# A first weight block on GpSimd's queue, and four small loads moved behind a weight chunk

## The chip, the cores and the metric

One core of a Trainium2 chip runs the whole kernel. The metric is device time in microseconds (us) of one execution. Before the change it was 484.42 us, the median of 3 runs (484.12 to 484.95).

The engines that matter here: TensorE (PE) multiplies, ScalarE (ACT) and VectorE (DVE) prepare its operands, SyncE (SP) and GpSimd (POOL) issue DMAs, each on a queue of its own.

## What is computed

One decoder layer on 256 positions of width 1024: an input projection feeds an mLSTM branch and an attention branch, both are gated, summed and projected, and a gated MLP follows. The start of the kernel, where the change sits, computes the output gate `o` of the mLSTM branch and the input and forget gate columns, which are columns of the input projection:

```python
proj = jnp.einsum("bsd,dn->bsn", x, w_in) + b_in
q_m, k_m, v_m, o_m, i_m, f_m, q_b, k_b, v_b, g_a, g_b = _split_cols(proj, SPLIT_SIZES)
...
y_a = (jax.nn.sigmoid(o_m.astype(jnp.float32)) * head_norm(h_m, mlstm_norm)).astype(x.dtype)
...
bias_own = jnp.moveaxis(rel_bias[t5_bucket(rel_own)], -1, 0).astype(jnp.float32)
```

## The kernel before

Float32 precision is reached by splitting every operand into a high part (`h`, type fp32r, a cast on ACT, line 93) and a low part (`l`, the rest, a subtraction on DVE, line 94) and multiplying three times: high by high, low by high, high by low (`split_into` and `mm3`). So every weight and input block goes through four hands: a DMA, ACT, DVE, PE.

The weights come as chunks of 1 MB (`wst[s]`, 128 x 2048), in the order of `chunk_order`: chunks 0 to 3 are the output gate's, then from chunk 4 on the projections of the queries, keys and so on (4 is the first queries' chunk, `qm`; 5 is `qb`, 6 `km`, 7 `kb`), and after 36 chunks of projections and gates come those of the later stages. `load(s)` issues the whole chunk s on SP's queue into one of three rotating buffers `raw`; `split_parts(s)` cuts it into high and low tiles `wh`, `wl`; `step_<kind>` multiplies.

The output gate is special, because nothing is loaded yet when it starts. Its four chunks and the transposed input are loaded in pieces, in the order in which PE uses them, in a loop over the eight slices k of 128 input features. For each k: one slice of the input (`xraw`, 128 KB); one piece of chunk 2 (into the tile `sgb`) and one of chunk 3 (into `sigo`), each 128 KB for k = 0 to 3 and 256 KB for k = 4 and 6; and one block of 256 KB of chunk 0 or 1 (into `raw`; for chunk 1 the split halves are called `yah` and `yal`). PE computes in `step_o`, for each k, the products of chunk 2's piece (`ps_o2a`, `ps_o2b`), chunk 3's with the gate columns `wif` (`ps_o3a`, `ps_o3b`) and the 512 columns of chunk 0 or 1 (`ps_o0a`, `ps_o0b`); for k = 0 and 1 in that order. ACT and DVE work through the casts and subtractions in a fixed order too, so a late piece holds up those behind it.

SP issues DMAs strictly in order. Its DMAs share eight completion semaphores (`DMAHW0` to `DMAHW7` in the rows below), so from the ninth on each waits for the landing of one about eight places ahead of it. POOL's queue has semaphores of its own (`DMASW`).

Behind the loop POOL broadcasts two bias rows (`bo`, `bvm`, lines 251 and 252), which wait for a load of SP's queue, and then issues four small loads: `rel` (the bias table, 2 KB as loaded), `onehot` (64 KB), `ident` (the identity for transposes, 64 KB) and `vec` (biases, convolution taps and gains, 138 KB). After them SP loads chunks 4 to 8.

`rel_split` casts `rel` and `onehot` (lines 283 to 285). From them `rel_bias_expand` makes, by one matmul (`ps_rel`, line 558), a table of the relative position bias in DRAM (`ev`, lines 562 and 563, then `table`), which is read back as `toe` for the attention's logits (line 777). `side_pe[s]` holds small PE work that is run right behind step s, `side_elem[s]` small ACT and DVE work that `elem_work(s)` runs ahead of step s. `vec` is first used by ACT at line 463, `ident` by the transposes into `ps_gt` (line 585).

Of the kernel before, what the change touches and what calls it, by code (L numbers as in the profile page):

```python
# [19 lines left out]
S = 256  # L20
# [52 lines left out]
class Kernel:  # L73
# [105 lines left out]
    def run(self):  # L179
        tc, nc, ctx = self.tc, self.nc, self.ctx  # L180
# [29 lines left out]
        ident = const.tile([P, P], F32, name="ident")  # L210
        vec = const.tile([P, NV], F32, name="vec")
        rel = xp.tile([2 * NB, 8], F32, name="rel")
        onehot = xp.tile([2 * NB, S], F32, name="onehot")
# [13 lines left out]
        raw = [self.stream.tile([P, 2048], F32, tag="raw", name=f"raw{s}", bufs=3) for s in range(2)]  # L227
# [6 lines left out]
        dma = nc.sync.dma_start  # L234
        cut = [(k // 4, slice(k % 4 * 512, k % 4 * 512 + 512)) for k in range(KT)]
        pieces = {0: 1, 1: 1, 2: 1, 3: 1, 4: 2, 6: 2}
        for k, (s, c) in enumerate(cut):
            dma(xraw[:, k], self.xt_d[:, k])
            for t in (2, 3, s) if k < 2 else (2, s, 3):
                if t == s:  # L240
                    dma(raw[s][:, c], self.wst[s, :, c])
                elif k in pieces:
                    d = slice(k * 256, (k + pieces[k]) * 256)
                    dma(raw[t][:, d], self.wst[t, :, d])
                if t == 3 and k == 0:
                    dma(self.wif, self.wif_d)
            if k == 3:

                dma(brow.rearrange("p (a d) -> p a d", a=2), self.rows_d[0:2, :].unsqueeze(0))
                dma(bif, self.bif_d.to_broadcast([P, 8]))  # L250
        nc.gpsimd.partition_broadcast(bo, brow[:, 0:D])
        nc.gpsimd.partition_broadcast(self.bvm, brow[:, D:2 * D])
        twice = (2, NB)
        for t, d in ((rel, self.rel_d.unsqueeze(0).to_broadcast([*twice, 8])),
                     (onehot, self.onehot_d[:, 0:S].unsqueeze(0).to_broadcast([*twice, S])),
                     (ident, self.ident_d), (vec, self.vec_d)):
            nc.gpsimd.dma_start(t, d)


        v3 = [t.rearrange("p (k f) -> p k f", k=KT) for t in whl[3]]  # L260
        for k, (s, c) in enumerate(cut):
# [4 lines left out]
            d = slice(k * 256, (k + n) * 256)  # L266
# [12 lines left out]
        both = xp.tile([2 * NB, 8], F32R, name="relhl")  # L279
        oneh = self.ybl.rearrange("p k s -> p (k s)")[0:2 * NB, 0:S]  # L280
# [6 lines left out]
        for s in range(4, 9):  # L287
            if s == 7:
                self.split(4)
            self.load(s)  # L290
        g = nc.gpsimd


# [27 lines left out]
        self.pst = {}  # L321


        self.rel_bias_expand(both, oneh)
        self.gates_schedule(bif)
        for gi in range(NG):
            self.group_schedule(gi)
# [7 lines left out]
        ffn_cm = tc.tile_pool(name="ffn", bufs=1)  # L335
        ahead_cm = tc.tile_pool(name="ahead", bufs=1, side="right")
        first = {k: self.order.index((k, 0)) for k in ("wa", "wo", "up")}
        for f in [self.gate_sums] + self.o_sums + [rel_split]:
            f()
        self.split(5)  # L340
        for s, (kind, i) in list(enumerate(self.order))[4:]:
# [207 lines left out]
        self.step_gate(s, "gb", g, V_BGB)  # L549


    def rel_bias_expand(self, rel, onehot):
        nc = self.nc
        st = {}

        def pe():
            st["ps"] = ps = self.ps_side([8, S], "ps_rel")
            nc.tensor.matmul(ps, rel, onehot, start=True, stop=True)

        def elem():  # L560
            ev = self.xp.tile([8, LTOE], F32, name="ev")
            nc.vector.tensor_scalar(ev[:, P:LTOE], self.backward(st["ps"]), 1.0 / ATT_SCALE, None, op0=ALU.mult)
            nc.vector.memset(ev[:, 0:P], NEG)
            nc.gpsimd.dma_start(self.table, ev)
            self.load_band(0)
        self.side_pe.setdefault(4, []).append(pe)
        self.side_elem.setdefault(5, []).append(elem)


    def gates_schedule(self, bif):  # L570
# [727 lines left out]
```

## Time and profile before

| | before |
|---|---|
| median of 3 runs | 484.42 us |
| the profiled execution | 485.31 us |
| its span, first to last instruction | 483.6 us |
| PE busy | 474.1 us |
| granted TensorE clock | 0.995 |

The time of the profiled execution is 1.7 us longer than its span: what lies ahead of the first and behind the last instruction. Rows of the timeline give the start in us, the duration, the engine, the line of the code, the operation with output and input tiles, and in square brackets how long the engine had stood idle just before and what released it. `SPq` is SP issuing a DMA. Tiles of one name are told apart by time: `raw` is the tile of chunk 0 before 11 us, of chunk 1 until 25 us, of chunk 4 behind that.

### The profile page before, as it was taken

To read this page: it belongs to the slowest core of one execution; us is meant where nothing else is said; L and a number is where in the kernel's file an instruction comes from. 1 tells how busy PE (TensorE), PEld (TensorE's weight loads), DVE (VectorE), ACT (ScalarE), POOL (GpSimd) and SP (SyncE) were. 2 spreads that over 40 slices of the span, in tenths; PEclk is the share of its full clock that TensorE was granted. 3 is DMA by queue.
4 is the path that set the end of the run, shared out by engine and by line. 5 is a ranking of instruction groups with operands and counts; after the bars stand their busy time and mean duration, and the time that the engine had idled before them with its cause. 6 is when DMAs were issued, how large, how long until landed. Compare 5 with 4: busy or idle time off the path is not lost.

```text
span 483.6 us, 9414 instructions
## 1 busy us (share of the span) xinstructions
PE 474.1 (98%) x3831; PEld 458.8 (95%) x3831; DVE 371.1 (77%) x666; ACT 297.9 (62%) x509; POOL 23.7 (5%) x41
## 2 busy tenths in 40 slices
PE   7999999999999999999999999999999999999994
PEld 5989999999999999999999999999999999999984
DVE  5779986886689668986677798888768767767886
ACT  5479777586667756866655632767456544555871
POOL 0500002000100010002000001000000000000000
PEclk9999999999999999999999999999999999999998
DMA  7976655364637453743954491837454655456202
GB/s 226 286 303 223 220 198 197 127 237 170 192 103 264 175 169 114 272 170 106 380 219 173 175 344 41 298 102 260 176 194 166 232 194 182 172 205 222 90 1 89
DMA packets 18214, 92.70 MB, mean 192 GB/s; under 512 B 2475, under 2 KB 5433, under 8 KB 8313
## 3 DMA queue, kind: packets, MB, share of 16 engines
q1 hardware_dynamic: 16714, 87.61, 50.3%
q0 software_dynamic: 1456, 4.49, 3.4%
q8 instruction: 30, 0.49, 0.4%
q14 instruction: 14, 0.11, 0.1%
HBM read 91.02 MB, written 1.06 MB: 190 GB/s over the span
## 4 chain that ended last, share of the span: by engine, by line
PE 92%; DMA 5%; DVE 1%; ACT 1%; SPq 1%; issue 0%; DVEq 0%; ACTq 0%
PE ps_up L147 25%; PE ffn L147 13%; PE ps_ga L147 5%; PE ps_kb L147 5%; PE ps_qb L147 5%; PE ps_gb L147 5%; PE ps_vm L147 5%; PE mix L147 5%; PE ps_vb L147 5%; PE ps_wb L147 5%; PE ps_wa L147 5%; PE ps_km L147 4%; PE ps_qm L147 4%; DMA raw<-in_wst_dram 2%; DMA sigo<-in_wst_dram 1%; PE psn L147 1%
## 5 line engine op out<-in xcount | busy, mean ns | idle before, releaser
L94 DVE TENSOR_TENSOR wl<-raw,wh 128x1024 fp32r<-128x1024 f32 (+4 forms) x147 | 180.3, 1264 | 26.3 <-ACT wh L93 23.5
L93 ACT CAST wh<-raw 128x1024 fp32r<-128x1024 f32 (+4 forms) x147 | 151.6, 1080 | 7.9 <-DMA raw<-in_wst_dram 5.6
L147 PE MATMUL ps_up<-x1h,wl 128*128 128x256 f32 x320 | 88.5, 276 | 0.0
L147 PE MATMUL ps_up<-x1h,wh 128*128 128x256 f32 x320 | 88.5, 276 | 0.0
L147 PE MATMUL ps_up<-x1l,wh 128*128 128x256 f32 x320 | 88.4, 276 | 0.0
L147 PEld LDWEIGHTS ps_up<-x1l,wh 128*128 128x128 f32 x320 | 60.1, 188 | 0.4
L147 PEld LDWEIGHTS ps_up<-x1h,wh 128*128 128x128 f32 x320 | 60.1, 188 | 0.3
L147 PEld LDWEIGHTS ps_up<-x1h,wl 128*128 128x128 f32 x320 | 60.1, 188 | 0.0
L1076 DVE SCALAR_TENSOR_TENSOR cu<-ps_up,vec,cu 128x255 f32<-128x255 f32 (+1 forms) x80 | 33.1, 476 | 20.4 <-ACT cu L1072 20.4
L147 PE MATMUL ffn<-wh,hl 128*128 128x512 f32 (+2 forms) x94 | 35.5, 378 | 0.0
L147 PE MATMUL ffn<-wl,hh 128*128 128x512 f32 (+2 forms) x94 | 35.5, 377 | 0.0
L147 PE MATMUL ffn<-wh,hh 128*128 128x512 f32 (+2 forms) x94 | 35.3, 375 | 0.0
L93 ACT CAST hh<-cu 128x256 fp32r<-128x256 f32 x22 | 8.9, 406 | 40.4 <-DVE cu L1087 40.4
L1072 ACT ACTIVATE cu<-ps_up,vec 128x256 f32<-128x256 f32 x40 | 16.7, 469 | 22.5 <-PE ps_up L147 22.5
L147 PEld LDWEIGHTS ffn<-wh,hl 128*128 128x128 f32 x94 | 17.7, 188 | 3.2
L147 PEld LDWEIGHTS ffn<-wl,hh 128*128 128x128 f32 x94 | 17.7, 188 | 3.1
L147 PEld LDWEIGHTS ffn<-wh,hh 128*128 128x128 f32 x94 | 17.7, 188 | 3.0
L147 PE MATMUL ps_qm<-xth,wl 128*128 128x256 f32 x64 | 17.9, 280 | 0.4 <-DVE wl L94 0.4
L147 PE MATMUL ps_qm<-xth,wh 128*128 128x256 f32 x64 | 18.0, 281 | 0.0
L147 PE MATMUL ps_ga<-xth,wh 128*128 128x256 f32 x64 | 18.0, 281 | 0.0
L147 PE MATMUL mix<-wh,mgh 128*128 128x256 f32 x64 | 17.8, 279 | 0.0
L147 PE MATMUL ps_qb<-xth,wh 128*128 128x256 f32 x64 | 17.8, 278 | 0.0
(343 smaller groups left out, 1444.6 us busy)
## 6 DMA issues: line engine op xcount, KB each, us to landing
raw<-in_wst_dram SPq DMA_DIRECT2D x77, 1024.0 KB, 4.9
raw<-in_wst_dram SPq DMA_DIRECT2D x8, 256.0 KB, 4.4
lnrow<-in_rows_dram POOLq DMA_DIRECT2D x4, 512.0 KB, 7.0
xraw<-in_xt_dram SPq DMA_DIRECT2D x8, 128.0 KB, 4.0
toe<-table POOLq DMA_DIRECT2D x4, 256.0 KB, 5.3
xtok<-in_x_dram POOLq DMA_DIRECT2D x1, 1024.0 KB, 8.1
sgb<-in_wst_dram SPq DMA_DIRECT2D x4, 128.0 KB, 3.9
sigo<-in_wst_dram SPq DMA_DIRECT2D x4, 128.0 KB, 3.7
```

The lines of the kernel that those rows point to most:

```text
L93: self.nc.scalar.copy(wh, raw)
L94: self.nc.vector.tensor_sub(wl, raw, wh.bitcast(F32))
L147: self.nc.tensor.matmul(ps, a[i], b[i], start=start and i == 0, stop=stop and i == 2)
L1072: act.activation(cu[:, j, :], ps[:, j, :], AF.Copy, scale=tap(2, j))
L1076: v.scalar_tensor_tensor(cu[:, j, o:], ps[:, j, :S - o], tap(t, j), cu[:, j, o:], op0=ALU.mult, op1=ALU.add)
```

## The change

Three edits. The block of k = 0 of chunk 0 (256 KB) is issued by POOL instead of SP. The four small loads leave POOL's queue: SP issues `vec` and `ident` behind chunk 4 and `rel` and `onehot` behind chunk 5. And, as `rel` and `onehot` come later, `rel_split` moves from ahead of step 4's loop into `elem_work(4)`, the matmul of `ps_rel` from behind step 4 to behind step 5, and the table's evacuation from step 5 to step 6.

```diff
             for t in (2, 3, s) if k < 2 else (2, s, 3):
                 if t == s:
-                    dma(raw[s][:, c], self.wst[s, :, c])
+                    (dma if k else nc.gpsimd.dma_start)(raw[s][:, c], self.wst[s, :, c])
...
         twice = (2, NB)
+        small = [(vec, self.vec_d), (ident, self.ident_d)]
         for t, d in ((rel, self.rel_d.unsqueeze(0).to_broadcast([*twice, 8])),
-                     (onehot, self.onehot_d[:, 0:S].unsqueeze(0).to_broadcast([*twice, S])),
-                     (ident, self.ident_d), (vec, self.vec_d)):
-            nc.gpsimd.dma_start(t, d)
+                     (onehot, self.onehot_d[:, 0:S].unsqueeze(0).to_broadcast([*twice, S]))):
+            small.append((t, d))
...
             self.load(s)
+            if s < 6:
+                for _ in range(2):
+                    dma(*small.pop(0))
...
-        self.rel_bias_expand(both, oneh)
+        self.rel_bias_expand(both, oneh, rel_split)
...
-        for f in [self.gate_sums] + self.o_sums + [rel_split]:
+        for f in [self.gate_sums] + self.o_sums:
             f()
...
-        self.side_pe.setdefault(4, []).append(pe)
-        self.side_elem.setdefault(5, []).append(elem)
+        self.side_elem.setdefault(4, []).append(split)
+        self.side_pe.setdefault(5, []).append(pe)
+        self.side_elem.setdefault(6, []).append(elem)
```

What it moves, at three places. First SP's queue at the very start; `raw0` is the tile of chunk 0. Before:

```order
L238 DMA xraw_88<-in_xt_dram 128x256
L244 DMA sgb_101<-in_wst_dram 128x256
L244 DMA sigo_106<-in_wst_dram 128x256
L246 DMA wif_98<-in_wif_dram 128x64
L241 DMA raw0_107<-in_wst_dram 128x512
L238 DMA xraw_88<-in_xt_dram 128x256
L244 DMA sgb_101<-in_wst_dram 128x256
L244 DMA sigo_106<-in_wst_dram 128x256
L241 DMA raw0_107<-in_wst_dram 128x512 [waits DMAHW0_49]
```

The same place on SP with the change:

```order
L238 DMA xraw_88<-in_xt_dram 128x256
L244 DMA sgb_101<-in_wst_dram 128x256
L244 DMA sigo_106<-in_wst_dram 128x256
L246 DMA wif_98<-in_wif_dram 128x64
L238 DMA xraw_88<-in_xt_dram 128x256
L244 DMA sgb_101<-in_wst_dram 128x256
L244 DMA sigo_106<-in_wst_dram 128x256
L241 DMA raw0_107<-in_wst_dram 128x512
L238 DMA xraw_88<-in_xt_dram 128x256 [waits DMAHW0_49]
```

The fifth DMA is gone from SP's list and everything behind it stands one place further ahead. It now heads POOL's list, in front of the broadcasts, and the four small loads are gone from there:

```order
L241 DMA raw0_107<-in_wst_dram 128x512
L251 ISA
L251 ISA bo_91<-sga_100 128x1024 [waits DMAHW0_49]
L252 ISA bvm_92<-sga_100 128x1024
L264 COPY xfirst_99<-xth_89 128x128 [waits Activation_49]
```

Second, SP's queue at the end of the output gate's loads, where the last block of chunk 1 (`raw1`) is followed by the chunks 4, 5, 6; with the change:

```order
L241 DMA raw1_108<-in_wst_dram 128x512 [waits DMAHW5_49]
L88 DMA raw4_358<-in_wst_dram 128x2048 [waits DMAHW6_49]
L293 DMA vec_95<-in_vec_dram 128x276 [waits DMAHW7_49]
L293 DMA ident_94<-in_ident_dram 128x128 [waits DMAHW0_49]
L88 DMA raw5_362<-in_wst_dram 128x2048 [waits DMAHW1_49,DMASW0_49,DVE_49]
L293 DMA rel_96<-in_rel_dram 64x1x8 [waits DMAHW2_49]
L293 DMA onehot_97<-in_onehot_dram 64x1x256 [waits DMAHW3_49]
L88 DMA raw6_366<-in_wst_dram 128x2048 [waits DMAHW5_49,DMAHW4_49,DVE_49]
```

Before, chunks 4, 5 and 6 stood here one behind the other; the four L293 rows are new.

Third, PE behind step 4 (`ps_qm0` is chunk 4's product, `ps_qb0` chunk 5's). Before:

```order
L147 MATMUL ps_qm0_437<-xth_89,wl4_369 128x256
L558 MATMUL ps_rel_486<-ybl_105,relhl_211 8x256 [waits DVE_49,PE_49,Activation_49]
L585 MATMUL ps_gt_488<-ident_94,gt_411 4x128 [waits DMASW2_49,PE_49]
L585 MATMUL ps_gt_488<-ident_94,gt_411 4x128 x3
L147 MATMUL ps_qb0_526<-xth_89,wh5_421 128x256 [waits Activation_49]
L147 MATMUL ps_qb0_526<-xtl_90,wh5_421 128x256
L147 MATMUL ps_qb0_526<-xth_89,wl5_422 128x256 [waits DVE_49]
```

With the change:

```order
L147 MATMUL ps_qm0_437<-xth_89,wl4_369 128x256
L589 MATMUL ps_gt_486<-ident_94,gt_411 4x128 [waits DMAHW0_49,DVE_49]
L589 MATMUL ps_gt_486<-ident_94,gt_411 4x128 [waits DVE_49]
L589 MATMUL ps_gt_486<-ident_94,gt_411 4x128 x2
L147 MATMUL ps_qb0_519<-xth_89,wh5_418 128x256 [waits DVE_49,PE_49,Activation_49]
L147 MATMUL ps_qb0_519<-xtl_90,wh5_418 128x256
```

The matmul of `ps_rel` has left this place; it stands 48 matmuls later, between chunk 5's and chunk 6's products. The lines behind the diff's third place are numbered three or four higher in the changed kernel.

More of the change, by code (lines that the diff above doesn't have):

```diff
@@ L549, in step_gb, with rel_bias_expand @@
         self.step_gate(s, "gb", g, V_BGB)
-    def rel_bias_expand(self, rel, onehot):
+    def rel_bias_expand(self, rel, onehot, split):
         nc = self.nc
```

## The prediction

> **What bounds the kernel now.** The page first: busy times, the chain that ended last, and the costliest issues.
>
> ```profile
> PE 474.1 (98%) x3831; PEld 458.8 (95%) x3831; DVE 371.1 (77%) x666; ACT 297.9 (62%) x509; POOL 23.7 (5%) x41
> ...
> PE 92%; DMA 5%; DVE 1%; ACT 1%; SPq 1%; issue 0%; DVEq 0%; ACTq 0%
> ```
>
> PE is busy 98% of the span and carries 92% of the chain. So the question is where PE stands still. The view of waits, asked for PE alone, answers with three rows for the whole execution:
>
> ```profile
> PE warm_ps L201 <- DVE warm L198: 1.3, 1, 1.3
> PE ps_o0a L427 <- ACT wh L93: 1.2, 1, 1.2
> PE ps_qm L147 <- DVE wl L94: 0.4, 1, 0.4
> ```
>
> The first is the start, which the change doesn't touch. The other two, 1.2 and 0.4 us, both lie in the first 31 us and are all that earlier loads can win. After the second, PE runs without a wait until its last product; time won or lost by then is carried to the end unchanged. The timeline shows the first wait:
>
> ```profile
> 2.65 0.43 SPq L241 DMA_DIRECT2D raw<-in_wst_dram  x1
> 4.55 0.40 ACT L93 CAST wh<-sigo 128x256 fp32r<-128x256 f32 x1
> 5.82 0.29 PE L427 MATMUL ps_o3b<-wl,xth 128*128 128x264 f32 x1
> 6.61 0.62 ACT L93 CAST wh<-raw 128x512 fp32r<-128x512 f32 x1 [1.66 <-DMA raw<-in_wst_dram]
> 7.29 0.50 PE L427 MATMUL ps_o0a<-wh,xth 128*128 128x512 f32 x1 [1.18 <-ACT wh L93]
> ```
>
> The block of k = 0, issued by SP at 2.65 as its fifth DMA, lands at about 6.6; ACT has waited 1.66 for it and PE starts 0.68 after the cast starts. This is the block that POOL is to load. What comes behind is tight as well, as the chain of waits says, which runs backward through DMAs, not PE, up to 27 us:
>
> ```profile
> 3.13 3.82 DMA xraw<-in_xt_dram
> ...
> 11.68 6.08 DMA sigo<-in_wst_dram
> ...
> 18.15 9.20 DMA raw<-in_wst_dram
> ...
> 29.58 1.23 DVE wl L94
> ```
>
> Each landing lets SP issue the next of these. The last is chunk 4, landing at 27.35; its last low half is ready at 30.81 and PE, which has arrived 0.35 earlier, goes on at 30.85. So a gain at 7.29 is kept only if the blocks between and chunk 4 come earlier too.
>
> **The block of k = 0.** SP's first issue, and the first DMA that POOL issues before:
>
> ```profile
> 0.81 0.38 SPq L238 DMA_DIRECT2D xraw<-in_xt_dram  x1
> 14.51 1.00 POOL L257 DMA_DIRECT2D rel<-in_rel_dram  x1
> ```
>
> A common start releases all engines, so I take 0.8 us for POOL's issue too. The landing on POOL's queue at that time is not in the trace, so it is bounded, from the views of DMA issues in narrow windows (the last figure is us from issue to landing):
>
> ```profile
> raw<-in_wst_dram SPq DMA_DIRECT2D x1, 256.0 KB, 3.9
> toe<-table POOLq DMA_DIRECT2D x1, 256.0 KB, 3.7
> vec<-in_vec_dram POOLq DMA_DIRECT2D x1, 138.0 KB, 7.1
> rel<-in_rel_dram POOLq DMA_DIRECT2D x1, 2.0 KB, 6.0
> ```
>
> The best case is `toe`, as large and on POOL's queue, at 48 us, when few loads were under way: 0.8 + 3.7 = 4.5. The worst is `vec`, on the same queue in the thick of the loads: 0.8 + 7.1 = 7.9. The nearest row is the block itself, which took 3.9 on SP's queue among these very neighbours. I add the longer issue of POOL's first DMA, 1.00 - 0.43 = 0.57: 0.8 + 3.9 + 0.57 = 5.3. Then PE could go on at 5.3 + 0.68 = 6.0, right behind the row at 5.82, and the wait of 1.18 is gone.
>
> Not all of it is taken. The 16 DMA engines are shared, and this is how busy they were (windows view; the last two columns are the DMA share and GB/s):
>
> ```profile
> 2.00:4.50 2.50, 2.50 (x8) 1.03 (x6) 0.84 (x2) 1.00 (x4) 0.00 (x0) 1.00 0.81 212
> 4.50:5.60 1.10, 1.10 (x11) 1.09 (x10) 0.66 (x3) 0.45 (x2) 0.00 (x0) 1.00 0.68 148
> 5.60:12.40 6.80, 5.62 (x36) 4.89 (x35) 4.62 (x11) 4.59 (x12) 0.33 (x1) 1.00 0.93 310
> 17.10:27.40 10.30, 10.30 (x67) 9.24 (x66) 5.75 (x10) 5.13 (x10) 1.14 (x8) 1.00 1.03 350
> ```
>
> Free engine time is 0.19 x 2.5 + 0.32 x 1.1 = 0.83 us ahead of 5.6; the block needs 256 KB at 310 GB/s, 0.85 us. It about fits, but while it runs it takes turns with `sigo`, whose cast at 4.55 leads to products at once. I take off 0.3: **a gain of 0.9 us at this place**, between 1.2 (all) and a loss of 7.9 + 0.68 - 7.29 = 1.3.
>
> The Trainium skill, in "DMA: Bandwidth & Descriptors", section "Issuing engines are not separate DMA queues", says that DMAs of several issuing engines run on the same 16 DMA engines, so that issuing from more of them saves only the sequencer's time. The shares of 0.81 and 0.68 above agree that the engines were largely taken; the issue time saved is one slot, 3.13 - 2.65 = 0.48 us, and by the rule alone the sum here would be 0.48 in place of 0.9. The same page's fit for a DMA of this queue (section "Anatomy of one DMA — SWDGE (gpsimd) path") would give, as an estimate, 2.0 + 0.6 = 2.6 us to landing; the 3.7 of `toe` is longer and is used.
>
> **Does the gain hold?** Every later piece is issued a slot of 0.48 earlier, and 0.83 us of engine time is newly used ahead of 5.6, so I take 0.7 us for the landings behind, between 0 and 0.83. The tight ones, and the row that frees a buffer for chunk 6:
>
> ```profile
> 17.07 0.62 ACT L93 CAST yah<-raw 128x512 fp32r<-128x512 f32 x1 [1.99 <-DMA raw<-in_wst_dram]
> 17.89 0.39 PE L427 MATMUL ps_o0a<-yah,xth 128*128 128x512 f32 x1
> 24.71 0.69 DVE L94 TENSOR_TENSOR wl<-sigo,wh 128x512 fp32r<-128x512 f32 x1 [1.27 <-ACT wh L93]
> 25.46 0.39 PE L427 MATMUL ps_o3a<-wl,xth 128*128 128x264 f32 x1
> 25.66 0.69 DVE L94 TENSOR_TENSOR yal<-raw,yah 128x512 fp32r<-128x512 f32 x1
> ```
>
> At k = 4 the high half is ready at 17.69 and used at 17.89: 0.20 to spare, and 0.20 + 0.7 = 0.9 carries just the gain. At k = 6 the low half is ready at 25.40 and used at 25.46, hardly anything; here the second edit helps.
>
> **The small loads leave POOL's queue.** Between 17.1 and 27.4 the DMA engines are full (share 1.03 above). The DMA view of that stretch, its row on POOL's queue:
>
> ```profile
> q0 software_dynamic: 256, 0.28, 11.4%
> ```
>
> Its 11.4% of 10.3 us is 1.17 us of all engines ahead of chunk 4's landing. Moved behind chunk 4, they free this time: chunk 4 lands 0.7 + 1.17 = 1.9 us earlier (between 0.5 and 2.0), more than PE's 0.9 + 0.35 = 1.25, so the second wait goes too: **0.35 us**. The blocks of k = 6 get most of the 1.17, enough for the 0.9.
>
> What the moved loads now collide with. Their users, and the work that moves:
>
> ```profile
> 29.45 0.19 ACT L283 CAST relhl<-rel 64x8 fp32r<-64x8 f32 x1
> 29.55 0.40 ACT L284 CAST ybl<-onehot 64x256 fp32r<-64x256 f32 x1
> 35.16 0.84 ACT L463 ACTIVATE cbuf<-ps_qm,vec 128x256 f32<-128x256 f32 x2 [0.31 <-PE ps_qm L147]
> 35.27 0.60 PE L585 MATMUL ps_gt<-ident,gt 128*4 128x128 f32 x4
> 38.24 0.61 DVE L465 TENSOR_SCALAR cvqm<-cbuf,vec 128x256 f32<-128x256 f32 x2
> 44.06 0.41 DVE L562 TENSOR_SCALAR ev<-ps_rel 8x256 f32<-8x256 f32 x1
> 45.89 0.61 DVE L505 SCALAR_TENSOR_TENSOR qbl<-ps_qb,vec,qbh 128x128 fp32r<-128x128 f32 x2 [0.72 <-ACT qbf L503]
> 48.08 0.77 POOL L406 DMA_DIRECT2D toe<-table  x1 [2.63 <-DMA table<-ev]
> 65.50 0.28 DVE L777 CUSTOM_DVE_ANT_0 lg<-psl,toe 128x128 f32<-128x128 f32 x1
> ```
>
> `vec` and `ident`, 202 KB behind chunk 4, are there by about 28 even if chunk 4 stays at 27.35, six us ahead of their use. They delay chunk 5 by 0.6 us at 350 GB/s, against 1.9 won, and its product starts only behind the row at 35.27. `rel` and `onehot` (66 KB, 0.2 us) stand ahead of chunk 6, whose issue waits for a buffer that DVE frees at 25.66 + 0.69 = 26.35; their own waits, for landings of k = 6, end earlier. SP's four more issues cost some 4 x 0.43 of its time, in which it would stand waiting for buffers.
>
> `rel_split`'s casts (0.19 and 0.40 on ACT) come behind chunk 6's and ahead of the row at 35.16, which may start 0.3 us later than PE allows; DVE uses its result only from 38.24, so nothing reaches PE. `ev` goes from 44.06 to behind the row at 45.89, to 46.5. `toe` landed at 48.08 + 3.7 = 51.8, 7.7 behind `ev`; it will at 54.2, still 11 us ahead of 65.50. All at nothing; without that cover `toe` would hold PE up. PE's `ps_rel` product is only moved.
>
> **The sum**: 0.9 + 0.35 = 1.25 us. The profiled execution, 485.31 = 483.6 + 1.7 around the span, would be 484.1; it lay 0.9 above the median of the runs, and from the median 484.42 it is **483.2 us**.
>
> **The rivals.** *The engines, not the issue, are the limit* (a mechanism of its own): the block takes its turns from `sigo` and `wif`, and the landings at k = 4 move by 0.2 only. Then 0.20 + 0.2 at k = 4 holds PE to 0.4 there, and chunk 4 gives 0.1 to 0.35: 0.5 to 0.75 us, 483.8. For it: shares of 0.81 and 0.93. Against: 148 GB/s in the window from 4.5, half of the next. Chance 0.29.
>
> *POOL's queue is slow to start*, the other side: the block lands as `vec` or `rel` did, or with a first issue that is longer than 1.00. It decides from a landing at 6.6, where the old wait is back; past 6.9 even the 0.35 from chunk 4 is eaten. At 7.9 the loss is 1.3 - 0.35 = 0.95: 485.4. For it: 6.0 us for the 2 KB of `rel`. Against: those waited among engines that were full, at 0.8 us nothing is in flight. Chance 0.08 in all, 0.05 past the 0.2% below.
>
> *Everything closes*: no loss to `sigo`, all small delays around k = 6 and chunk 4 vanish: 1.2 + 0.35 + 0.3 = 1.9, 482.5. Chance 0.11. That the block isn't loaded earlier at all, the change not doing what it says, is the landing at 6.6 in the second rival.
>
> **How the numbers follow.** The forecast has 0.52. A measurement of this kernel can tell about 0.2%, 0.97 us, from no change. Of the forecast 0.43 lies past 0.97, and with the last rival's 0.11 faster has 0.54; slower 0.05; the rest, 0.41, is within. The range runs from everything closed, 482.5, to a late block that loses 0.4: 484.8.
>
> **What would show it.** PE's waits: the row of 1.2 gone or under 0.4, that of `ps_qm` gone, no new one. The cast of the first `raw` starting near 5.3; near 6.6 or later speaks for the second rival. The cast of the `raw` of k = 4 at 16.4, not 16.9. Chunk 4's cast near 25.6. The prediction is wrong if PE waits at k = 4 or 6 for what it no longer waits for at k = 0, or if a product behind 35 us waits for `vec`, `ident` or `toe`.

## The result and the profile after

The changed kernel took 488.1 us, the median of 6 runs (487.02 to 488.49), against 484.46 of the kernel before in 6 runs (484.12 to 484.95): a ratio of 1.0066, 95% interval 1.0051 to 1.0081. In a later comparison it took 486.70 (4 runs, 486.55 to 486.95) against 484.78: 1.0043 (1.0026 to 1.0060). Forecast were 483.2 and a range that ends at 484.8. It is slower, and by more than any rival allowed.

The profiled execution took 487.05 us, its span 485.3. Its busy line, the chain's shares, and all of PE's waits:

```profile
PE 474.8 (98%) x3831; PEld 459.8 (95%) x3831; DVE 371.1 (76%) x666; ACT 297.9 (61%) x509; POOL 22.1 (5%) x38
...
PE 97%; DMA 1%; DVE 0%; ACT 0%; SPq 0%; issue 0%; DVEq 0%; ACTq 0%
```

```profile
PE ps_o3a L430 <- ACT wh L93: 1.5, 1, 1.5
PE warm_ps L201 <- DVE warm L198: 1.3, 1, 1.3
```

The two waits that were to go, 1.2 and 0.4, are gone. A new one of 1.5, at `ps_o3a`, takes their place, so PE waits as long as before. It is also busy 0.7 us longer for the same 3831 products, and no wait shows why. Where the 1.7 us of span came from, by the start of the first product of each stage in both timelines:

| from - to | before | after | difference |
|---|---|---|---|
| start - first `ps_qm` | 28.60 | 29.41 | +0.81 |
| `ps_qm` - `ps_qb` (chunk 4's stage) | 7.02 | 5.80 | -1.22 |
| `ps_qb` - `ps_km` | 5.55 | 5.84 | +0.29 |
| `ps_km` - first `ps_ga` (km, kb, vm, vb) | 24.00 | 24.91 | +0.91 |
| `ps_ga` - first store of the last rows | 414.40 | 414.23 | -0.17 |
| that store - end of the span | 3.99 | 5.12 | +1.13 |

Each column is one execution. A second profile was taken of each kernel (`h2_before_again` and `h1_after_again`, below). These two differ by 1.65 us in span, in part at other places: +0.15 at the start, -0.59 from `ps_qm` to `ps_km`, +0.92 from `ps_km` to `ps_ga` and +1.16 at the end. So the slower stages and the late end are there both times, and the loss at the start mostly is not.

**The start.** The timeline of after. The block of k = 0 heads POOL's list, and three casts of ACT and a product of PE show what it did:

```profile
1.33 0.76 POOL L241 DMA_DIRECT2D raw<-in_wst_dram  x1 [0.82 <-POOLq L1291]
...
6.88 0.24 ACT L93 CAST wh<-wif 128x64 fp32r<-128x64 f32 x1 [2.78 <-DMA wif<-in_wif_dram]
7.03 0.40 ACT L93 CAST wh<-sigo 128x256 fp32r<-128x256 f32 x1
7.34 0.62 ACT L93 CAST wh<-raw 128x512 fp32r<-128x512 f32 x1
...
7.49 0.40 PE L430 MATMUL ps_o3a<-wh,xth 128*128 128x264 f32 x1 [1.48 <-ACT wh L93]
```

Before, ACT cast `sigo` at 4.55 and `raw` at 6.61. Now the casts of `wif` and `sigo`, which SP still issues at 2.17 and 1.70, start only at 6.88 and 7.03, and everything of k = 0 comes at once. The block had its landing 5.1 us behind its issue, at 6.4. The DMA view from 3.0 to 4.5 us, by queue, of after and then of before (packets, MB, share of the 16 engines; q0 is POOL's, q1 SP's):

```profile
q0 software_dynamic: 48, 0.18, 62.1%
q1 hardware_dynamic: 107, 0.08, 16.8%
```

```profile
q1 hardware_dynamic: 381, 0.31, 81.0%
```

SP's queue, with the small rows that are needed first, fell from 81.0% of the engines to 16.8%. POOL's queue moved 3.7 KB a packet, SP's 0.75 KB. The second profile agrees in kind, 14.6% for SP's queue, with the cast of `sigo` at 6.57 and a shorter wait of PE:

```profile
PE ps_o3a L430 <- ACT wh L93: 0.9, 1, 0.9
```

**The slower pace.** The chain of work of after, and of before, in the stages from 41 us (start, length, 48 products each):

```profile
41.12 5.85 PE ps_km L147 x48
46.97 5.65 PE ps_kb L147 x48
52.62 5.65 PE ps_vm L147 x48
58.28 5.65 PE ps_vb L147 x48
```

```profile
41.33 5.44 PE ps_km L147 x48
46.77 5.47 PE ps_kb L147 x48
```

The same products, on the same tiles, with no wait ahead of any, take 5.65 us instead of 5.45: 0.1177 us each against 0.1133. The slower pace begins at the new place of `ps_rel` and ends with the stage of vb. Only its mean tells it from waiting: no product stands out.

**The end.** SP's waits from 476 us on, of after and of before; L1298 and L1294 are the end of the program:

```profile
SPq L1298 <- DMA out_dram<-x: 1.5, 1, 1.5
SPq L1298 <- PEq L1298: 1.2, 2, 1.0
```

```profile
SPq L1294 <- DMA out_dram<-x: 1.2, 3, 0.5
SPq L1294 <- PEq L1294: 0.7, 2, 0.5
```

The last store lands 2.0 us behind its issue in both. What grew lies behind it, where SP looks at its completion semaphores one by one.

### The profile page after: what moved, and what is told of

It reads as the page before. It is cut to its first block, busy times and chain, and to the rows that moved or that the text cites. A ratio compares the mean times of both kernels' runs of the same rounds, so it can differ in the third digit from the quotient of the medians.

```text
span 485.3 us, 9411 instructions
## 1 busy us (share of the span) xinstructions
PE 474.8 (98%) x3831; PEld 459.8 (95%) x3831; DVE 371.1 (76%) x666; ACT 297.9 (61%) x509; POOL 22.1 (5%) x38
## 4 chain that ended last, share of the span: by engine, by line
PE 97%; DMA 1%; DVE 0%; ACT 0%; SPq 0%; issue 0%; DVEq 0%; ACTq 0%
PE ps_up L147 25%; PE ffn L147 12%; PE ps_km L147 5%; PE ps_kb L147 5%; PE ps_vm L147 5%; PE ps_vb L147 5%; PE ps_ga L147 5%; PE ps_gb L147 4%; PE ps_qb L147 4%; PE ps_qm L147 4%; PE mix L147 4%; PE ps_wb L147 4%; PE ps_wa L147 4%; PE ps_o0b L430 1%; PE ps_o0a L430 1%; DMA wif<-in_wif_dram 1%
## 5 line engine op out<-in xcount | busy, mean ns | idle before, releaser
L147 PE MATMUL ps_km<-xth,wh 128*128 128x256 f32 x64 | 17.8, 279 | 0.0
```

What stands on the lines that cost most here:

```text
L147: self.nc.tensor.matmul(ps, a[i], b[i], start=start and i == 0, stop=stop and i == 2)
```

## The experiments

### One part of the change at a time

`e1_block_pool` is the kernel before with only the block on POOL's queue; `e2_tables_only` is the change without that edit; `e3_rel_back` is the change with `ps_rel`, its split and its evacuation at their old steps, and so all four small loads behind chunk 4:

```diff
-            if s < 6:
-                for _ in range(2):
+            if s < 5:
+                for _ in range(4):
...
-        for f in [self.gate_sums] + self.o_sums:
+        for f in [self.gate_sums] + self.o_sums + [rel_split]:
...
-        self.side_elem.setdefault(4, []).append(split)
-        self.side_pe.setdefault(5, []).append(pe)
-        self.side_elem.setdefault(6, []).append(elem)
+        self.side_pe.setdefault(4, []).append(pe)
+        self.side_elem.setdefault(5, []).append(elem)
```

> Only the first edit: the block of k = 0 on POOL's queue, the small loads and the table's work as before. Theory A (the block takes the DMA engines' turns from sigo and wif at k = 0, so PE stands still ahead of ps_o3a, and the clock opens later): the wait of about 1.5 us ahead of ps_o3a is there as in the changed kernel, the executions spread as the changed kernel's do, with clocks of 0.992 and 0.995, and the time is 485.5 to 488. Theory B (the loss comes from the moved product ps_rel and the pace behind it): km to vb run at 5.44 to 5.47 us each and the time is within 0.2% of before.

> Only the second and third edits: the small loads behind chunks 4 and 5 on SP, rel_split and ps_rel moved, the block of k = 0 on SP as before. Theory A: PE waits 1.2 us at k = 0 as before, the wait for chunk 4 is gone, executions agree within 0.2%, the time is 483.5 to 484. Theory B: km, kb, vm and vb take 5.65 us each in place of 5.45, which eats the gain: 484.3 to 485.

> The changed kernel with ps_rel, rel_split and the evacuation back at steps 4 and 5, and all four small loads behind chunk 4. Theory B: km to vb run at 5.45 us each and the profiled span is about 0.9 us shorter than that of the changed kernel, 484.4, still with the wait ahead of ps_o3a. Theory A alone: the chunks' pace is as in the changed kernel, and the time too, 487 to 488.5.

| | median us (before 484.82) | ratio, 95% | first `ps_qm` against before | km to vb | store to end |
|---|---|---|---|---|---|
| e1 | 485.52 (11 runs) | 1.0019 (1.0010 to 1.0028) | +0.13 | 24.0 | 4.4 |
| e2 | 486.35 (5) | 1.0034 (1.0022 to 1.0046) | +0.34 | 24.9 | 4.9 |
| e3 | 486.25 (6) | 1.0037 (1.0024 to 1.0050) | +0.41 | 24.0 | 5.1 |

No part alone gains. The third column tells little: ten profiles of kernels with the block on SP's queue and at full clock, e2's among them, have the first `ps_qm` between 28.60 and 28.98, and with the block on POOL's queue it lies at 28.73 (e1), 28.92 (h1), 29.01 (e3) and 29.41 (the first profile of the changed kernel; e5 and f2, below, have 29.55 and 30.70, with more products and with a slow clock). What is steady is the late cast of `sigo`, at 6.37 to 7.08 in the six profiles with the block on POOL's queue and at 4.5 to 5.2 with it on SP's; PE's wait at `ps_o3a` is 0.7 in e1 and 1.2 in e3. Of the 0.7 us by which e1 is slower, 0.4 lies at the end.

The slower pace goes with `ps_rel`'s place: there in e2, gone in e3, whose chain reads

```profile
40.82 5.44 PE ps_km L147 x48
46.26 5.47 PE ps_kb L147 x48
```

But e3 still ends late, by 5.1 us from store to end, so that is a cause of its own.

### The first block on ACT's queue

```diff
-                    (dma if k else nc.gpsimd.dma_start)(raw[s][:, c], self.wst[s, :, c])
+                    (dma if k else nc.scalar.dma_start)(raw[s][:, c], self.wst[s, :, c])
```

> The changed kernel with the block of k = 0 issued by ACT's hardware queue instead of POOL's; nothing else differs. If it is the kind of POOL's queue that held up sigo and wif (landed 6.88 us with the block on POOL's queue, 4.4 to 4.6 before), they land before 5.4 us here, PE's wait at ps_o3a (1.5 us with the change) falls under 0.5, the first queries' stage starts 0.3 to 0.5 us earlier than with the change and the time falls by about 0.5 us from that of the changed kernel. If any block of 256 KB that runs beside them takes their turns, sigo and wif land after 6 us again, the wait stays above 1 us and the time stays within 0.3 us of the changed kernel's. The slower matmul pace behind ps_rel (0.1175 us from start to start until about 64 us) and the late end stay in both cases.

485.70 us (10 runs) against 484.76, ratio 1.0015 (1.0006 to 1.0023). PE's waits are down to the one of the start, and the DMA view from 3.0 to 4.5 us has SP's queue at work beside ACT's (q10):

```profile
PE warm_ps L201 <- DVE warm L198: 1.3, 1, 1.3
```

```profile
q1 hardware_dynamic: 447, 0.33, 66.2%
q10 hardware_dynamic: 75, 0.12, 30.3%
```

The casts of `wif` and `sigo` start at 5.11 and 5.26 (`sigo` 0.7 later than before), that of `raw` at 5.57, within 0.3 us of the 5.3 that the forecast wanted. The first `ps_qm` starts at 27.92 (28.19 in the two other kernels with the block on ACT's queue, f3 and g1), ahead of all profiles with the block on SP's or POOL's queue: 1.5 us ahead of the first profile of the changed kernel and 1.0 ahead of the second. The time fell by 1.0 us from the 486.70 of the changed kernel, twice what was expected. The block is also issued 0.53 earlier (0.80 on ACT, 1.33 on POOL), and no run has both queues at the same issue time, so how much of this is the kind of queue is not settled; if the earlier issue is worth its own 0.5, it is 0.5 to 1.0. So the bytes nearly fit beside the others, as the forecast worked out; from POOL's queue they did not let the others through. The Trainium skill, in "DMA: Bandwidth & Descriptors", section "SWDGE vs HWDGE vs iDMA", says that in each DMA engine the software and the hardware path feed different internal queues and the engine takes them in turn. The rows agree that POOL's and SP's queues shared the engines, but not evenly: 48 packets and 0.18 MB of POOL's went against 107 and 0.08 of SP's. Of ACT's queue, a hardware queue as SP's is, 75 packets and 0.12 MB went against 447 and 0.33. What a turn holds is not shown here.

### What sets the pace

`f1_rel_only` moves only `ps_rel` and its evacuation in the kernel before. `f2_transposes_behind` is the changed kernel with four transposes more right behind `ps_rel`:

```diff
+        def again():
+            ps = self.ps_side([4, 2, S], "ps_gt")
+            ...
+        self.side_pe.setdefault(5, []).append(again)
```

> The kernel before, in which only the product of ps_rel (to behind step 5) and its evacuation (to step 6) are moved; every load stays. If the place of ps_rel is what puts PE into the slower pace, the matmuls of km, kb, vm and vb take 0.1178 us from start to start, PE is 0.2 to 0.3 us later with each of these stages, ends about 0.9 us later and the time is about 485.7 (before 484.8). If it takes more than that (the early chunk 4, a missing wait), the pace stays 0.1133 and the time 484.8, within 0.3.

> The changed kernel, with four transposes more behind the product of ps_rel (those of ps_gt once again, into a PSUM tile that nothing reads); PE has 0.45 us of work more. In the fast kernels the stream of pairs was entered behind four such transposes, in the changed one behind ps_rel itself. If what stands right ahead of the stream picks the pace, km to vb go at 0.1133 us, PE gains 0.9 and loses 0.45, and the time is 0.3 to 0.6 us under the changed kernel's (about 486.6 where that gives 487.0). If the pace is not picked there, it stays at 0.1178 and the time is 0.4 us above the changed kernel's.

f1 took 485.87 us, ratio 1.0024 (1.0014 to 1.0034): moving this one product of 0.28 us, with its evacuation, costs 1.1 us. (Its profiled execution took 496.72 us, so its stages are not used.) f2 took 486.58 us (6 runs) against 484.73. Its chain:

```profile
42.94 5.46 PE ps_km L147 x48
48.40 5.47 PE ps_kb L147 x48
```

The pace is back at 0.1133 although PE has some 0.45 us more to do, and the time is at or under the 486.70 of the changed kernel. So in these kernels `ps_rel` right ahead of the stream of pairs of weight load and product brings the slower pace, and four transposes between them take it away. Every other profile with `ps_rel` right ahead of `ps_km` has 5.65 us a stage: the two of the changed kernel, e2, e4 and e5. But it is not the only thing that brings it: in the profile of the kernel before, the products of chunk 4 behind PE's wait come 0.118 us apart, and in h2 0.113, behind the same wait. Why `ps_rel` alone leads into the slow pace stays open.

### The round of semaphores, first try

`e6_three_loads` adds three loads of 4 KB to the kernel before, into a new tile; `e8_sp_late` is e3 with the block back on SP and four such loads; `f4_three_loads_wif` is e6 with the old tile `wif` as target, behind the chunks 12 to 14. The edit of e6:

```diff
+        self.lane = const.tile([P, 3, 8], F32, name="lane")
...
+        if 14 <= s < 17:
+            self.nc.sync.dma_start(self.lane[:, s - 14], self.bif_d.to_broadcast([P, 8]))
```

> The kernel before, with three loads of 4 KB more on SP's queue, behind the chunks 14, 15 and 16 (near 100 us), into a tile that nothing reads; PE's work is that of the kernel before. Theory of the tail: three more hardware DMAs turn the round of eight completion semaphores by three, as the change does, and the last stores fall on semaphores that SP checks earlier or later in its list at the end; then PE ends within 0.15 us of the kernel before and the stretch from the first store's issue to the end of the span grows from 4.03 to about 5.1 us (5.11 with the change): the time rises by about 1.0 us, to 485.8. Rival: the late end is due to the work that the change moves and to how PE comes out of it; then the stretch stays at 4.0 and the time at 484.8, within 0.3.

> The changed kernel with the block of k = 0 back on SP, ps_rel, its split and its evacuation at their old steps, all four small loads on SP behind chunk 4, and four loads of 4 KB more behind the chunks 14 to 17 into a tile that nothing reads, so that SP issues eight DMAs more than before and the round of eight semaphores comes out as before. If the three losses are all that stood against the earlier chunk 4, PE ends 0.6 to 1.1 us earlier than before, the stretch at the end is 4.0 us and the time about 484.0. If the round of semaphores has nothing to do with the late end, the stretch is 4.9 to 5.1 as in the runs with these loads on SP, and the time 484.9 to 485.2.

> The kernel before with three loads of 4 KB more on SP's queue, behind the chunks 12 to 14, into wif's tile after its last reader; no tile moves in SBUF (in the run with the loads behind the chunks 14 to 16 all tiles behind a new one moved by 96 bytes, and PE ran at 0.120 us in the later gates). If the round of semaphores makes the late end, the stretch from the first store to the end of the span is 4.6 to 5.1 us instead of 4.03, with PE's end within 0.3 of before, and the time about 485.6 (before 484.8). If the moved tiles and not the loads made the slow pace, no long stretch of a pace over 0.115 shows here that the kernel before does not have; if the loads did, it shows again and the time is above 487.

All three failed as tests of the end: e6 took 488.52, e8 489.38, f4 492.69. In e6 and e8 the new tile moves all tiles behind it, by 96 and 128 bytes. Two rows of e6's chain, and two of the same stages in f4's, where no tile moves:

```profile
244.81 5.76 PE ps_wb L149 x48
250.57 5.76 PE ps_wa L149 x48
```

```profile
239.49 5.44 PE ps_wb L149 x48
244.93 5.44 PE ps_wa L149 x48
```

A third pace, 0.120 us, all through the stages `wa` and `wb`, which goes with the tiles' places and not with the loads. In e8 those stages run at 0.118, and so do `qb` to `vb`, although `ps_rel` is back at its old place:

```profile
40.99 5.65 PE ps_km L149 x48
46.64 5.65 PE ps_kb L149 x48
```

f4 lost its time elsewhere: ACT stood idle until the third added load landed, PE waited 3.9 us at `psn` for ACT, and then its clock was at half rate for 3.4 us (in the second row, of the windows view, the last three numbers are granted clock, DMA share and GB/s):

```profile
70.33 1.28 ACT L669 ACT_TABLE_LOAD   x1 [6.43 <-DMA wif<-in_bif_dram]
76.30:79.70 3.40, 3.40 (x18) 3.40 (x17) 3.37 (x11) 1.16 (x4) 0.00 (x0) 0.50 0.13 14
```

e8 ended late too, 5.1 us from store to end, though its last store has the same semaphore as before: its last stores took 2.6 us to land, not 2.0.

### The round of semaphores, second try

Chunk 20 is cut into four DMAs (three in g4); no byte and no tile more:

```diff
+        for c in [slice(i * 512, i * 512 + 512) for i in range(4)] if s == 20 else [slice(0, 2048)]:
+            self.nc.sync.dma_start(t[:, c], self.wst[s][:, c])
```

> The kernel before with chunk 20 loaded as four pieces of 256 KB instead of one DMA of 1 MB: three hardware DMAs more, no byte more, no tile moved; the last store falls on the semaphore that SP checks first, as in the changed kernel. If that makes the late end, the stretch from the first store to the end of the span is 4.8 to 5.1 us (before 4.03), PE ends within 0.3 us of before and the time is about 485.6 (before 484.7). If not, the stretch is 4.0 and the time 484.7.

> The same with three pieces: two hardware DMAs more, so that the last store falls on the semaphore that SP checks last. If the order of the list decides, the stretch at the end is 3.8 to 4.0 us and the time 484.5 to 484.8; if any three or two DMAs more cost something by themselves, both this run and the one before it come out about 0.5 to 1 us later.

g3 took 485.32 us (11 runs), ratio 1.0014 (1.0005 to 1.0023), with 4.87 from store to end; g4 484.95, 1.0003 (0.9994 to 1.0012), with 4.15. In both, 0.2 us of this lies behind the clearing of semaphores, where the other kernels do not have it (f4 does). The records of semaphore instructions behind the last store, which no view lists, grouped by the place of its semaphore in SP's list of eight, over all profiles:

```
place of the last store   landing to SP's end of list   kernels
8th                       0.08 us                       g1 g2 g4
6th                       0.20 to 0.23                  before e7 e8 f1 f3
5th                       0.62                          e1
2nd                       0.79 to 0.80                  e2 e4
1st                       0.86 to 0.88                  after e3 e5 e6 f2 f4 g3
```

g3 and g4 differ in one DMA alone and stand at the two ends of this table, so the place is the cause. The change issues three hardware DMAs more, which turns the last store from the 6th place to the 1st: 0.64 us. A second piece lies on POOL, between SP's end and the clearing of semaphores: 0.38 to 0.39 us in every kernel in which POOL issues at least two of the four small loads, 0.74 to 0.89 in all seven in which it issues none. That is 0.5 us for the change; why it goes with them was not tried. Together they make the 1.1 us by which the changed kernel ends late.

### The clock at the start, and the runs above 488

In three of the six first runs the changed kernel had a mean granted clock of 0.992 and took 488.14 to 488.49; a fourth took 488.06 at 0.995, and the profiled one has 0.995 too. `e5_keep_warm` adds five products without use between those of `ps_o2` and `ps_o3` of k = 0, so that PE does not idle:

```diff
+                if k == 0 and n == 1:
+                    for _ in range(5):
+                        mm(self.wps, self.warm[:, :P], self.warm, start=True, stop=True)
```

> The changed kernel with five more products of the warm-up tile put between ps_o2 and ps_o3 of k = 0, into the warm-up's bank, where PE stands still for 1.5 us; they compute nothing that is used. If the 1.1 to 1.4 us between the changed kernel's executions at 487.0 and those at 488.1 to 488.5 are a clock that opens later because PE stood still (theory C), all executions lie at 487.0 or below with clock 0.995 or more. If they come from elsewhere, both groups stay.

> The changed kernel once more, for a profile of its commoner, longer executions (488.1 to 488.5, clock 0.992; profiled so far: 487.05, clock 0.995). If in these the clock falls back to half for one stretch of 3.4 us behind PE's wait at ps_o3a, as the run with the transposes showed (0.51 between 7.5 and 11 us, with a mean of 0.992), a profile at 0.992 shows such a stretch near 7 to 11 us, the first queries' stage starts 1.0 to 1.5 us later than in the profile of 487.05 and the rest is as there. If it shows full clock from 6 us on, the extra 1 us comes from elsewhere. A profile at 0.995 tells nothing new.

e5 took 486.84 (5 runs, 486.56 to 487.20; clocks 0.995 to 0.997). That alone proves nothing: h1, the changed kernel itself, had no long execution either. What such an execution looks like was caught in f2's profile (487.94, clock 0.992; four of its six runs took 485.93 to 486.72; e3 has one such run, 488.03 at 0.993). Its windows (the last three columns are granted clock, DMA share, GB/s), and its wait:

```profile
4.00:7.50 3.50, 1.48 (x10) 1.08 (x9) 0.96 (x4) 0.98 (x4) 0.00 (x0) 1.00 0.90 244
7.50:11.00 3.50, 3.50 (x12) 3.01 (x12) 2.72 (x7) 2.49 (x8) 0.00 (x0) 0.51 0.92 292
11.00:14.00 3.00, 3.00 (x21) 2.73 (x21) 2.92 (x8) 2.71 (x7) 0.59 (x1) 1.00 0.81 260
```

```profile
PE ps_o3a L430 <- ACT wh L93: 2.0, 1, 2.0
```

PE is busy 1.48 of 3.5 us around the wait, and for the next 3.4 us its clock is 0.51: 12 products, where 23 fit in after's profile. The Trainium skill, "TensorE: Matmul & The Clock Gate", section "What's actually happening", has windows of 3.4 us that run freely, and half rate behind an idle one; the stretch has this length, and a free-running window would explain why only some executions have it. But PE was not idle in the 3.4 us ahead of the stretch, it was busy for 1.4 of them; in f4, ahead of its own stretch, for 1.05. At half rate 3.4 us lower the mean by 3.4 x 0.5 / 486 = 0.0035, which is 0.992 against 0.995. The run of 488.06 at 0.995 doesn't fit, and no trace of the changed kernel itself has the stretch, so that this is what made its longer executions is likely and not shown.

### Was there a wait to win at chunk 4?

`h2_before_again` is the kernel before, without an edit.

> The kernel before once more, for a profile nearer its median (484.4 to 484.7; the one at hand took 485.31). Seven profiles of kernels whose first 30 us load as before have the stage of chunk 4 shorter than the one at hand by 0 to 0.9 us. If the wait at ps_qm and the slower pace behind it belong to single executions, a profile near 484.5 lacks them and the stage from ps_qm to ps_qb takes 6.1 us instead of 7.02, so that the changed kernel had little to gain there. If a profile near 484.5 has the wait and 7.0 us, the gain was there to be had.

h2 gave 484.94 us (10 runs), its profile 484.92. Two of PE's waits in it:

```profile
PE ps_o0a L427 <- ACT wh L93: 0.9, 1, 0.9
PE ps_qm L147 <- DVE wl L94: 0.3, 1, 0.3
```

The stage from `ps_qm` to `ps_qb` takes 6.69 us, not 7.02. Of the kernels that load as before up to there, e6, f4 and g3 have no wait at `ps_qm` at all, though the stage starts within 0.1 us of h2's; in e6 and g3 it takes 6.13 and 6.10 us without the change, and 6.11 in g2 with the loads moved. In g4 it takes 6.72 with a wait of 0.3, in f4 6.51, with products 0.118 us apart. How long it takes differs from execution to execution, and the one on which the forecast rests was a long one in this very stage.

### Towards a better version

`e7_pool_late` only has POOL's four small loads behind a copy of a piece of chunk 4; `f3_act_and_late` adds the block on ACT's queue (and copies a smaller piece). `g2_two_behind` moves only `ident` and `vec` to SP; `g1_two_behind_act` is g2 with the block on ACT's queue:

```diff
             self.load(s)
+            if s == 4:
+                dma(ident, self.ident_d)
+                dma(vec, self.vec_d)
```

> The kernel before, in which only the four small loads are moved: they stay on POOL's queue but are issued behind a POOL copy of a piece of chunk 4, so after chunk 4 has landed; the block of k = 0 stays on SP and ps_rel at its old place. If the gain of the change is the earlier chunk 4 alone and its losses are the block on POOL, ps_rel's place and the three DMAs more on SP, then the wait at ps_qm (0.4) is gone, the matmuls keep 0.1133 us, PE ends 0.7 to 1.2 us earlier than before, the stretch at the end stays 4.0 us and the time falls to about 483.9 (before 484.8). Rival: the slower pace or a late end comes back without any of these (it would then belong to the missing wait at ps_qm); then the time is 484.6 to 485.8.

> The kernel before with two edits: the block of k = 0 is issued by ACT's hardware queue, and POOL issues its four small loads behind a copy of 16 columns of chunk 4 into the unused head of xfirst's tile; ps_rel stays, SP issues one DMA less and ACT one more. If the start gains 0.7 us as in the run with ACT's queue and chunk 4's stage 0.9 as in the run with the late loads, PE ends 1.3 to 1.7 us earlier than before, the end stays 4.0 us, and the time is about 483.3 (before 484.8). If the gains overlap, or PE falls into its slower pace on the way, the time is 484.0 to 485.0.

> The kernel before with the block of k = 0 on ACT's hardware queue and only ident and vec moved to SP's queue behind chunk 4; rel, onehot and ps_rel stay. The loads that move are 202 KB of the 268 KB. Two hardware DMAs more than before put the last store on the semaphore that SP checks last. If the changed kernel's losses are the block on POOL's queue, ps_rel's place and the semaphore of the last store, the first queries' stage starts 0.4 to 0.7 us earlier than before, chunk 4's stage gains 0.7 to 1.2, the stretch at the end is at most 4.0 us, and the time is about 483.2 (before 484.7). If chunk 5 is late for a PE that is ahead (0.8 us in the run with ACT's queue and the late loads on POOL), the time is 484.0 to 484.7.

> As the run before it, but the block of k = 0 stays on SP's queue: the loads' move alone. If the forecast for the loads holds without ps_rel's move and without the late end, chunk 4's stage gains 0.7 to 1.0 us, the stretch at the end is at most 4.0 us and the time is about 483.9 (before 484.7). If the end is 4.9 or more again, the place of the last store in SP's list is not its cause.

| | median us | before | ratio, 95% | PE at `ps_qb` against the first profile of before |
|---|---|---|---|---|
| e7 | 485.01 (12 runs) | 484.76 | 1.0008 (0.9999 to 1.0018) | -0.83 |
| f3 | 485.00 (12) | 484.73 | 1.0005 (0.9993 to 1.0016) | -1.16 |
| g2 | 484.45 (11) | 484.59 | 0.9995 (0.9986 to 1.0003) | -0.67 |
| g1 | 483.71 (11) | 484.59 | 0.9980 (0.9971 to 0.9988) | -1.32 |

g1 is faster than the kernel before, by 0.9 us, and so than the changed one. Its waits of PE, and of SP at the end:

```profile
PE warm_ps L201 <- DVE warm L198: 1.3, 1, 1.3
PE ps_o2a L429 <- ACT wh L93: 0.6, 1, 0.6
```

```profile
SPq L1296 <- DMA out_dram<-x: 0.7, 2, 0.4
SPq L1296 <- PEq L1296: 0.6, 2, 0.5
```

e7 missed its 483.9: its profiled execution (484.60) has neither the slower pace nor a late end, and why its median lies at 485.01 is not shown. In f3 all four loads run ahead of chunk 5, which is then late for a PE that is ahead: PE waits 0.8 us at `ps_qb`. g2 shows the moved loads alone, freed of the losses: 0.14 us, inside what a measurement can tell. Both g kernels leave `rel` and `onehot` with POOL and have their last store in the 8th place.

## Why the prediction was wrong

The forecast's terms against the second profiles of both kernels: a gain of 0.9 at the block, where 0.15 was lost; a gain of 0.35 at chunk 4, where 0.59 was won; nothing for `ps_rel`'s move and the end, where 0.92 and 1.16 were lost. So the steps that failed are the price of the block on POOL's queue and, larger, the two terms that were put at nothing.

- **POOL's issue.** Taken at 0.8, from a start that was thought common to all engines; measured 1.33 to 2.09. The landing was taken at 5.3; measured 6.4 (5.7 to 6.5 in the six profiles with the block on that queue). The cast of `raw` came at 7.34, 0.7 behind that of before. The step took the row of `raw` on SP's queue, 3.9 us, as nearest for POOL's first DMA, which took 4.4 to 5.1.
- **Turns taken from `sigo` and `wif`.** A term of 0.3; it was 2.5 us for `sigo` (4.55 to 7.03). This is the first rival's mechanism with a price that neither it nor the forecast had, since both shared by bytes and not by what each queue got. The rival had the engines as the limit; e4 shows that they were not.
- **Does the gain hold.** There was none to hold: `ps_qm` started 0.81 late in the first pair of profiles and 0.15 in the second. The cast of k = 4 came at 17.00, not 16.4; but it lies anywhere between 15.3 and 18.2 over all profiles, so it was no sign to go by.
- **The small loads.** Right in its signs: the wait at `ps_qm` is gone, no user of `vec`, `ident`, `rel` or `onehot` waits for them, and the stage got shorter by 0.93 us net of `ps_rel` (0.59 in the second pair), more than the 0.35 forecast. Chunk 4's cast starts at 26.45 (25.95 in h1) in place of 25.6. But by e6, g3 and g2 that stage takes 6.1 us with and without the moved loads, where nothing disturbs it, so that the median has little of the gain.
- **"PE's `ps_rel` product is only moved."** It moved, as said, from one stage to the next. Not foreseen were the 0.91 us behind it: f1 has 1.1 us for this move alone.
- **SP's four more issues** were put down as time in which SP waits anyway, and so they are at 20 us. With the block gone from SP they are three more hardware DMAs, which cost 0.64 us at the end of the program, and POOL's four small loads fewer came with 0.5: no step looked beyond PE's last product.
- **The clock** was read as full throughout. By f2, a longer wait at `ps_o3a` can bring 3.4 us at half rate, 1.7 us as an estimate, in some executions.
- **From the profile to the median.** The forecast took 1.25 off the median 484.42, though the waits were read in an execution 0.9 longer. Of that 0.9, 0.33 lies in chunk 4's stage itself, 7.02 against 6.69 in h2.

Of the miss of 4.9 us in the first comparison 1.25 are gains that did not come, 1.7 the losses in the profile's span, 0.9 the way from the execution of 485.31 to the median, and 1.05 the way from the execution of 487.05 to the median of 488.1. In the later comparison, 486.70 against 484.78, the loss is 1.9 us and the miss 3.2.

## What to carry to other kernels

A load that is moved to another queue changes the turns of all that run beside it: look at the share of each queue where the smallest, most urgent pieces land, and try ACT's queue before POOL's. Compare the busy time of the engine that bounds as well as its waits, since a stream can go into a slower pace without a wait, and compare the end of the program, which depends on how many DMAs were issued. A wait or a loss read from one execution is worth its place in the median only if a second profile has it: here the wait ahead of chunk 4 and most of the loss at the start were not steady.

## What the hardware showed unexpectedly

PE's stream of pairs ran at three steady paces on the same work and clock: 0.1133, 0.1177 and 0.120 us. The list of eight semaphores at the end cost between 0.08 and 0.88 us by the place of the last store. And a block of 256 KB left SP's queue 16.8% of the DMA engines when it ran on POOL's queue, 66.2% when it ran on ACT's.
